# The opening of an expert stage: tokens in weight buffers, small first chunks, other work queued behind the first rows

## The chip, the core and the metric

The kernel runs on one core of a Trainium2 chip. The metric is the device time of one execution in microseconds (us), the median over a few runs. The profile is that of one execution, with its own time beside its span. Engines are named as the profile names them: PE (TensorE matmul) and PEld (its weight loads), DVE (VectorE), ACT (ScalarE), POOL (GpSimd, which issues the gathers) and SP (which issues the other loads).

## The reference, cut to what matters

One token sequence (256 tokens of 1024 features) passes two layers of a mixed attention, recurrence and convolution block and then a third block, which ends with a layer of experts picked per token (`peer` in the reference). Only that last layer is touched:

```
h2 = rmsnorm(x, g_norm2) * (1 + sc2) + sh2                    # normed tokens
q = (h2 @ w_pq) -> 8 heads x 2 halves x 128;  s = q . sub_keys # scores, 128 keys per half
sv, si = top_k(s, 16);  best, pos = top_k(sv0 + sv1, 16)       # 16 experts of 16384 for each token and head
g = softmax(best);  a = gelu(expert_u[eidx] . h2)
x = x + gt2 * sum over heads and experts of g * a * expert_v[eidx]
```

Each token picks 8 x 16 experts, and each expert is a row of `expert_u` and one of `expert_v`, 1024 numbers each, laid side by side in one table `uv`.

## The kernel before, in words

The tokens are two blocks b of 128. A "row" is one gather: for head h, block b and rank k it fetches one `uv` row of 8 KB for each of the 128 tokens, 1 MB, into one of NG = 9 buffers `G` (L1685, POOL). There are 16 rounds r of 16 rows, 256 rows in all: first the eight heads of block 0, then those of block 1. For each row VectorE takes the dot product of its first half with the tokens `hn[b]` (L1689). After a chunk of rows (four, as a rule) ScalarE takes one gelu (L1693), VectorE multiplies by the gates, and for each row ScalarE makes a diagonal matrix `dg` of the weights (L1702) with which TensorE adds the second half of the row into four PSUM accumulators `vacc`: two matmuls of 512 columns in float32, which the profile records in two passes each. Only then is the row's buffer free for another gather.

The scores of a head (`scores`) are 48 matmuls of normed tokens and weights, both split into a rounded part and a rest (`hh` and `hl`, `wh` and `wl`; three products each); the rounded part is an ACT copy (L323), the rest a subtraction on DVE (L268). Weights come through five raw buffers `w` and three split ones. Head 0's scores are made ahead of the stage. `routing` picks the experts on DVE, in small steps that are slipped in between the dot products (`side`, `nside` steps for each row); that of head 0 and block 0 comes in two parts, so that the first eight rows can be asked for early.

What opens the stage, in `peer`: the first part of `routing(0, 0)`; `normed`, which makes the normed tokens in a gather buffer `G` and splits them into `hh` and `hl`; the rest of that routing; `natural`, which turns the tokens to token order by matmuls of `hh` and `hl` with the identity and copies them to `hn` (both blocks); `scores(1)`; `residual`, which transposes the input `XT` in place for the sum at the end, by way of the four PSUM banks in which `vacc` starts afterwards; and then the rounds, with `scores(r + 2)` ahead of each of the first six.

The order on each engine is a planner's. `at(us)` sets the due time of what follows; the planner plays the program through with its own estimates, and of what is ready on an engine takes the one that is due first, so that work due later fills idle places. `tc.issue_after(x)` puts an instruction behind x in that order. Weight loads are due 25 us and splits 6 us ahead of their matmuls; `first_splits` holds two subtractions behind a given instruction. Each engine then runs its list strictly in order.

## Time and profile before

| | us |
|---|---|
| median of three runs | 1377.39 |
| the runs | 1371.65 to 1379.26 |
| profiled execution | 1375.42 |
| its span | 1373.6 |

| engine | busy us | share of the span |
|---|---|---|
| PE | 1197.5 | 87% |
| DVE | 994.4 | 72% |
| ACT | 533.6 | 39% |
| POOL | 292.5 | 21% |

The page's slices put the stage of the experts in the second half of the span: POOL works only there, and the DMA share is at 9 tenths or more nearly throughout. The gathers move 268.45 MB of 387.64. Shares over the whole span say little of one stage; the rows below are of the stage itself. Times of a row are counted from the start of the span.

### The profile page before, as it was taken

To read this page: it belongs to the slowest core of one execution; us is meant where nothing else is said; L and a number is where in the kernel's file an instruction comes from. 1 tells how busy PE (TensorE), PEld (TensorE's weight loads), DVE (VectorE), ACT (ScalarE), POOL (GpSimd) and SP (SyncE) were. 2 spreads that over 40 slices of the span, in tenths; PEclk is the share of its full clock that TensorE was granted. 3 is DMA by queue.
4 is the path that set the end of the run, shared out by engine and by line. 5 is a ranking of instruction groups with operands and counts; after the bars stand their busy time and mean duration, and the time that the engine had idled before them with its cause. 6 is when DMAs were issued, how large, how long until landed. Compare 5 with 4: busy or idle time off the path is not lost.

```text
span 1373.6 us, 17829 instructions
## 1 busy us (share of the span) xinstructions
PE 1197.5 (87%) x6008; PEld 781.7 (57%) x6008; DVE 994.4 (72%) x2464; ACT 533.6 (39%) x1147; POOL 292.5 (21%) x279
## 2 busy tenths in 40 slices
PE   6999899899979999999889977778787877779877
PEld 5987559798947976758676633343333333323333
DVE  6898865599988676466588777777767677676554
ACT  5535643344755555455444312222222222212211
POOL 0000000000000000000033443434444444444442
PEclk8999999899999999999979999988999999998899
DMA  9587455557413442401399999999999999999996
GB/s 333 196 284 270 157 183 173 196 163 260 139 41 100 154 131 77 153 16 36 108 382 381 376 426 428 425 426 361 427 412 426 427 426 418 423 426 404 421 427 275
DMA packets 71483, 387.64 MB, mean 282 GB/s; under 512 B 8417, under 2 KB 9569, under 8 KB 38370
## 3 DMA queue, kind: packets, MB, share of 16 engines
q0 software_dynamic: 36864, 268.45, 46.9%
q1 hardware_dynamic: 34530, 118.06, 25.4%
q8 instruction: 48, 0.79, 0.2%
q14 instruction: 41, 0.34, 0.1%
HBM read 385.43 MB, written 1.05 MB: 281 GB/s over the span
## 4 chain that ended last, share of the span: by engine, by line
PE 49%; DMA 28%; issue 9%; DVE 8%; POOL 5%; ACT 2%; POOLq 0%; DVEq 0%; SPq 0%; ACTq 0%
DMA G<-uv,eix 23%; PE acc L256 22%; PE acx L256 10%; PE s L256 5%; POOL G L1685 5%; DVE G L1689 3%; PE o L256 2%; DMA wm<-wada 2%; PE c L256 2%; PE c L966 2%; PE t L256 1%; DMA w<-wpq 1%; PE t L259 1%; PE s L412 1%; PE o L645 1%
## 5 line engine op out<-in xcount | busy, mean ns | idle before, releaser
L1689 DVE SCALAR_TENSOR_TENSOR G<-G,hn 128x1024 f32<-128x1024 f32 x256 | 313.4, 1225 | 162.3 <-DMA G<-uv,eix 158.8
L1685 POOL DMA_INDIRECT G<-uv,eix x256 | 284.9, 1113 | 415.6 <-PE o L256 129.5
L323 ACT ACTIVATE wh<-w 128x1024 fp32r<-128x1024 f32 (+2 forms) x140 | 146.4, 1048 | 180.6 <-PE acc L256 111.0
L268 DVE TENSOR_TENSOR wl<-w,wh 128x1024 fp32r<-128x1024 f32 (+2 forms) x140 | 168.8, 1209 | 65.4 <-ACT wh L323 63.8
L256 PE MATMUL t<-G,dg 128*128 128x512 f32 x256 | 149.3, 668 | 62.9 <-ACT dg L1702 62.9
L256 PE MATMUL c<-G,dg 128*128 128x512 f32 x256 | 145.9, 654 | 49.2 <-ACT dg L1702 49.2
L256 PE MATMUL acc<-hh,wh 128*128 128x256 f32 x592 | 173.5, 297 | 6.0 <-ACT hh L468 2.5
L256 PE MATMUL acc<-hh,wl 128*128 128x256 f32 x592 | 173.0, 295 | 2.0 <-DVE wl L268 2.0
L256 PE MATMUL acc<-hl,wh 128*128 128x256 f32 x592 | 164.3, 288 | 1.1 <-DVE hl L268 1.1
L1702 ACT ACTIVATE dg<-cst,w 128x128 f32<-128x128 f32 x256 | 90.1, 395 | 141.7 <-PE acx L256 61.4
L256 PE MATMUL acx<-G,dg 128*128 128x512 f32 x256 | 143.3, 644 | 0.0
L256 PE MATMUL o<-G,dg 128*128 128x512 f32 x256 | 141.1, 635 | 0.0
L1693 ACT ACTIVATE s<-s 128x4 f32<-128x4 f32 (+1 forms) x66 | 13.5, 205 | 306.7 <-DVE G L1689 306.7
L256 PEld LDWEIGHTS t<-G,dg 128*128 128x128 f32 x256 | 50.9, 209 | 142.3 <-ACT dg L1702 87.6
L256 PEld LDWEIGHTS acc<-hh,wh 128*128 128x128 f32 x592 | 115.7, 196 | 14.8 <-issue 4.6
L256 PEld LDWEIGHTS acc<-hh,wl 128*128 128x128 f32 x592 | 115.9, 196 | 8.6 <-issue 4.3
L256 PEld LDWEIGHTS c<-G,dg 128*128 128x128 f32 x256 | 49.5, 206 | 117.0 <-ACT dg L1702 68.5
L262 DVE SCALAR_TENSOR_TENSOR g<-lu,pb,g 128x256 f32<-128x256 f32 x264 | 115.1, 478 | 0.2
L256 PEld LDWEIGHTS acc<-hl,wh 128*128 128x128 f32 x592 | 111.3, 192 | 5.3 <-issue 3.4
L256 PEld LDWEIGHTS acx<-G,dg 128*128 128x128 f32 x256 | 53.5, 209 | 70.7 <-issue 70.7
L256 PEld LDWEIGHTS o<-G,dg 128*128 128x128 f32 x256 | 52.7, 206 | 69.0 <-issue 68.8
L1057 POOL MEMSET lu<- 128x16 f32 x1 | 0.4, 441 | 399.3 <-DVE g L262 399.3
(549 smaller groups left out, 1998.6 us busy)
## 6 DMA issues: line engine op xcount, KB each, us to landing
w<-w SPq DMA_DIRECT2D x64, 512.0 KB, 4.4
wm<-wada SPq DMA_DIRECT2D x40, 512.0 KB, 4.3
wa<-cw SPq DMA_DIRECT2D x16, 512.0 KB, 5.0
w<-woa SPq DMA_DIRECT2D x16, 512.0 KB, 3.5
w<-wpq SPq DMA_DIRECT2D x14, 512.0 KB, 4.5
w<-w2t SPq DMA_DIRECT2D x12, 512.0 KB, 3.5
w<-wob SPq DMA_DIRECT2D x8, 512.0 KB, 3.5
w<-w2v SPq DMA_DIRECT2D x8, 512.0 KB, 3.8
```

Of the source, the lines that this page charges most:

```text
L256: return pe.matmul(out, lhsT, rhs, start=start, stop=stop)
L259: pe.transpose(out, in_, ident)
L262: return (e or dve).scalar_tensor_tensor(out, a, s, b, op0=op0, op1=op1)
L268: return (e or dve).tensor_tensor(out, a, b, op=op)
L323: act.activation(hi, w, AF.Copy)
L412: pe.matmul(acc[j:j + 32], ones[:, 0:32], sq[:, q] if square else srcs[i + q], start=i + q < 4, stop=i + q >= n - 4, tile_position=(0, j))
L645: pe.matmul(hps[32 * j:32 * j + 32], blk[:, q4 * 4 + j], w[:, j], start=q4 == 0, stop=q4 == 3, tile_position=(0, 32 * j))
L966: pe.matmul(acc[32 * j:32 * j + 32], sc[:, k], w[:, j], start=k == 0, stop=k == 7, tile_position=(0, 32 * j))
L1685: pool.indirect_dma_start(out=G, out_offset=None, in_=A["uv"], in_offset=bass.IndirectOffsetOnAxis(ap=eix[b][:, h, k:k + 1], axis=0))
L1689: dot = dve.scalar_tensor_tensor(G[:, 0:D], G[:, 0:D], 1.0, hn[b], op0=mul, op1=mul, accum_out=s[:, j:j + 1])
L1693: act.activation(s[:, 0:n], s[:, 0:n], AF.Gelu)
L1702: act.activation(dg, ident, AF.Copy, scale=w[:, j:j + 1])
```

## The change

`normed` now makes the tokens in two of the raw weight buffers `w` (no gather buffer) and adds the shift in place. `natural(0, tokens)` turns only block 0 for the first rows, by float32 transposes straight from these; block 1 follows at round 3 from `hh` and `hl`, as before. The split into `hh` and `hl` is a step of its own (`halves`): its copies are put behind the last copy of `natural`, its subtractions behind the second dot product. Round 0 has chunks of 2, 2, 4, 4, 4 rows instead of four of 4. `scores(1)` is put behind the last matmul of the first two rows and its two weight splits behind their weights; `scores(2)` is due 20 us after the start of the rounds, where it was due 12 us before. `residual` is done per block, before rounds 2 and 4, through the PSUM banks of the scores. No routing steps stand beside the first two rows, a routing that is unfinished at the end of a round may go on in the next if its head is not the next one, and round 1 has three steps for each row instead of two. `finish` reads the residual in its new layout.

```
@@ -1536,13 +1538,14 @@
         gat = [mk(pp, [128, 8, 16], tag=f"gat{b}") for b in range(2)]
         sca = mk(pp, [128, 7, 2, 2, 128], tag="sca")
 
-        def scores(h, t):
+        def scores(h, t, held=None):
 
             acc = pst("u", [128, 2, T])
             for q in range(2):
                 at(t + 2.6 * q)
                 wh, wl = wsplit(A["wpq"][2 * h + q], [128, 8, 128])
-                mm3(acc[:, q], [(wh[:, k], wl[:, k], hh[:, k], hl[:, k]) for k in range(8)])
+                with tc.issue_after(held.ins) if held else nullcontext():
+                    mm3(acc[:, q], [(wh[:, k], wl[:, k], hh[:, k], hl[:, k]) for k in range(8)])
             at(t + 5.2)
             qs = mk(pp, [128, 2, T], tag="qs", bufs=2)
             act.activation(qs, acc, AF.Copy)
@@ -1559,24 +1562,34 @@
                 dg = mk(pp, [128, 128], tag="dg", bufs=3)
                 ts(dg, ident, rs2[:, b:b + 1], None, mul)
                 mm(bc[:, b * 128:b * 128 + 128], ones, dg, True, True)
-            t = mk(pp, [128, 2 * D], tag="G", bufs=NG).rearrange("p (k t) -> p k t", k=8)
+            t = [mk(wp, [128, 4, 256], tag="w", bufs=NRAW) for _ in range(2)]
             for k in range(8):
-                stt(t[:, k], XT[:, k], mg["pr"][:, k:k + 1], bc, mul, mul)
-                sh = modt[:, 24 + k, 0:1]
-                act.activation(hh[:, k], t[:, k], AF.Identity, bias=sh)
-            for k in range(8):
-                stt(hl[:, k], t[:, k], modt[:, 24 + k, 0:1], hh[:, k].bitcast(F32), add, sub)
-
-        def natural():
-
-            for b in range(2):
-                for d in range(2):
-                    acc = pst("u", [128, 4, 128])
-                    for k in range(4):
+                o = t[k // 4][:, k % 4]
+                stt(o, XT[:, k], mg["pr"][:, k:k + 1], bc, mul, mul)
+                act.activation(o, o, AF.Identity, bias=modt[:, 24 + k, 0:1])
+            return t
+
+        def halves(t, a, d):
+            for k in range(0, 8, 2):
+                src = t[k // 4][:, k % 4:k % 4 + 2]
+                with tc.issue_after(a):
+                    act.activation(hh[:, k:k + 2], src, AF.Copy)
+                with tc.issue_after(d):
+                    tt(hl[:, k:k + 2], src, hh[:, k:k + 2].bitcast(F32), sub)
+
+        def natural(b, t=None):
+
+            bs = slice(b * 128, b * 128 + 128)
+            for d in range(2):
+                acc = pst("u", [128, 4, 128])
+                for k in range(4):
+                    if t is None:
                         for i, x in enumerate((hh, hl)):
-                            last = mm(acc[:, k], x[:, d * 4 + k, b * 128:b * 128 + 128], identr, i == 0, i == 1)
-                    act.activation(hn[b][:, d * 512:d * 512 + 512], acc.rearrange("p a b -> p (a b)"), AF.Copy)
-            return last
+                            mm(acc[:, k], x[:, d * 4 + k, bs], identr, i == 0, i == 1)
+                    else:
+                        tr(acc[:, k], t[d][:, k, bs], ident)
+                copied = act.activation(hn[b][:, d * 512:d * 512 + 512], acc.rearrange("p a b -> p (a b)"), AF.Copy)
+            return copied
 
         def subscores(h, b, p):
             return sca0[:, b, p] if h == 0 else sca[:, h - 1, b, p]
@@ -1655,17 +1668,15 @@
             yield ts(g, g, sm, None, mul)
 
 
-        xn = XT.rearrange("p k t -> p (k t)").rearrange("p (b d) -> p b d", b=2)
-
-        def residual(held):
-            xp = [pst("v", [128, 4, 128]) for _ in range(4)]
-            for b in range(2):
-                for k in range(8):
-                    with tc.issue_after(held.ins):
-                        tr(xp[b * 2 + k // 4][:, k % 4], XT[:, k, b * 128:b * 128 + 128], ident)
-            for i in range(4):
-                act.activation(xn[:, i // 2, (i % 2) * 512:(i % 2) * 512 + 512],
-                               xp[i].rearrange("p a b -> p (a b)"), AF.Copy)
+
+        def residual(b):
+
+            for d in range(2):
+                xp = pst("u", [128, 4, 128])
+                cells = XT[:, 4 * d:4 * d + 4, b * 128:b * 128 + 128]
+                for k in range(4):
+                    tr(xp[:, k], cells[:, k], ident)
+                act.activation(cells, xp, AF.Copy)
 
         vacc = []
         side = []
@@ -1692,17 +1703,26 @@
                     if j == n - 1:
                         act.activation(s[:, 0:n], s[:, 0:n], AF.Gelu)
                         w = mk(pp, [128, 4], tag="w4", bufs=3)
-                        tt(w[:, 0:n], s[:, 0:n], gat[b][:, h, c:c + n], mul)
+                        gated = tt(w[:, 0:n], s[:, 0:n], gat[b][:, h, c:c + n], mul)
                     with tc.issue_after(dot.ins):
-                        for _ in range(nside):
+                        for _ in range(nside if h or b or c else 0):
                             while side and next(side[0], 0) == 0:
                                 side.pop(0)
+                if h == 0 and b == 0 and c == 0:
+
+                    at(t + 6)
+                    halves(tokens, copied.ins, dot.ins)
+                    first_splits.extend([gated.ins] * 2)
                 for j, G in enumerate(rows):
                     dg = mk(pp, [128, 128], tag="dg", bufs=3)
                     act.activation(dg, ident, AF.Copy, scale=w[:, j:j + 1])
                     for d in range(2):
-                        mm(vacc[b * 2 + d], dg, G[:, D + d * 512:D + d * 512 + 512], h == 0 and c + j == 0,
-                           h == 7 and c + j == 15)
+                        last = mm(vacc[b * 2 + d], dg, G[:, D + d * 512:D + d * 512 + 512], h == 0 and c + j == 0,
+                                  h == 7 and c + j == 15)
+                if h == 0 and b == 0 and c == 0:
+                    scores(1, t + 8, last)
+                if h == 0 and b == 0 and c == 4:
+                    scores(2, t + 20)
                 c += n
 
         PICK, NG = 2.5, 9
@@ -1716,17 +1736,13 @@
 
         at(B + 2)
         with tc.issue_after(found.ins):
-            normed()
-        at(B + 7)
+            tokens = normed()
+        at(B + 3)
         with tc.issue_after(found.ins):
             for ins in fast:
                 placed = ins
-        at(B + 8)
-        held = natural()
-        first_splits.extend([found.ins] * 2)
-        scores(1, B + 9)
-        at(B + 16)
-        residual(held)
+        at(B + 4)
+        copied = natural(0, tokens)
 
         gtb = mk(pp, [128, 2, 512], tag="gtb")
         gs = mk(pp, [128, D], tag="gs")
@@ -1749,22 +1765,37 @@
                 o = fin[:, d * 512:d * 512 + 512]
                 tt(o, vacc[b * 2 + d], gtb[:, d], mul)
                 yield 1
-                tt(o, o, xn[:, b, d * 512:d * 512 + 512], add)
+                o4 = o.rearrange("p (k n) -> p k n", k=4)
+                tt(o4, o4, XT[:, 4 * d:4 * d + 4, b * 128:b * 128 + 128], add)
                 nc.sync.dma_start(A["out"][b * 128:b * 128 + 128, d * 512:d * 512 + 512], o)
                 yield 1
 
+        route = {}
         for r in range(16):
-            nxt = [routing(q % 8, q // 8) for q in ((1, 2) if r == 0 else (r + 2,)) if q < 16]
-            side[0:0] = nxt
             if r == 3:
                 side.append(gate_sums())
             if r == 10:
                 side.append(finish(0))
-            if r < 6:
-                scores(r + 2, U0 + 16 * PICK * r - 12)
-            experts(r % 8, r // 8, U0 + 16 * PICK * r, 4 if r == 0 else 2, (4, 4, 4, 4) if r < 15 else (4, 4, 4, 2, 1, 1))
-            at(U0 + 16 * PICK * (r + 1))
-            while side and (side[0] in nxt or r in (6, 12)):
+            for q in (1, 2) if r == 0 else (r + 2,):
+                if q < 16:
+                    route[q] = routing(q % 8, q // 8)
+            side[0:0] = [route[q] for q in (r + 1, r + 2) if q in route]
+            t = U0 + 16 * PICK * r
+            if r in (2, 4):
+                at(t)
+                residual(r // 2 - 1)
+            if r == 3:
+                at(t)
+                natural(1)
+            if 0 < r < 6:
+                scores(r + 2, t - 12)
+            experts(r % 8, r // 8, t, 4 if r == 0 else 3 if r == 1 else 2, (2, 2, 4, 4, 4) if r == 0 else (4, 4, 4, 4) if r < 15 else (4, 4, 4, 2, 1, 1))
+            at(t + 16 * PICK)
+            ahead = route.pop(r + 1, None)
+            for _ in ahead or ():
+                pass
+            side[:] = [x for x in side if x is not ahead and x not in route.values()]
+            while side and r in (6, 12):
                 for _ in side.pop(0):
                     pass
         at(U0 + 16 * PICK * 16 + 20)
```

## Rows read from the trace of the kernel before

**Rows 1.** The page's chain that ended last, shares of the span by engine and line.
```profile
DMA G<-uv,eix 23%; PE acc L256 22%; PE acx L256 10%; PE s L256 5%; POOL G L1685 5%; DVE G L1689 3%; PE o L256 2%; DMA wm<-wada 2%; PE c L256 2%; PE c L966 2%; PE t L256 1%; DMA w<-wpq 1%; PE t L259 1%; PE s L412 1%; PE o L645 1%
```

**Rows 2.** Stretches: us; busy time (instructions) per engine; granted TensorE clock; DMA share; GB/s.
```profile
688.00:704.00 16.00, 10.30 (x45) 9.73 (x45) 15.86 (x53) 5.93 (x15) 8.44 (x8) 0.50 0.98 398
716.00:728.00 12.00, 12.00 (x49) 6.98 (x48) 10.98 (x48) 6.27 (x13) 5.71 (x5) 1.00 0.92 327
744.00:764.00 20.00, 20.00 (x95) 13.10 (x94) 12.87 (x36) 7.01 (x13) 8.33 (x8) 1.00 0.97 374
768.00:780.00 12.00, 12.00 (x49) 7.14 (x49) 9.01 (x25) 3.85 (x9) 4.63 (x4) 1.00 0.81 307
800.00:850.00 50.00, 39.43 (x86) 16.34 (x85) 35.90 (x96) 10.77 (x29) 22.84 (x21) 0.96 1.01 427
920.00:940.00 20.00, 18.18 (x60) 9.72 (x59) 13.57 (x37) 6.63 (x15) 6.97 (x6) 0.91 0.83 323
```

**Rows 3.** Timeline of POOL: start, length, line, operation, [idle before <-releaser]; one row per gather.
```profile
686.95 1.41 POOL L1685 DMA_INDIRECT G<-uv,eix  x1 [35.47 <-PE t L256]
...
704.36 1.18 POOL L1685 DMA_INDIRECT G<-uv,eix  x1 [5.78 <-issue]
...
718.40 1.86 POOL L1685 DMA_INDIRECT G<-uv,eix  x1 [12.86 <-PE o L256]
...
727.29 0.94 POOL L1685 DMA_INDIRECT G<-uv,eix  x1 [0.78 <-DVE sv L1621]
...
734.37 1.55 POOL L1685 DMA_INDIRECT G<-uv,eix  x1 [1.28 <-PE o L256]
```

**Rows 4.** Timeline of DVE, from the first index to that of head 1.
```profile
685.71 0.17 DVE L262 SCALAR_TENSOR_TENSOR eix<-ij 128x8 uint32<-128x8 f32 x1
...
686.19 3.49 DVE L268 TENSOR_TENSOR wl<-w,wh 128x1024 fp32r<-128x1024 f32 x3
...
689.60 0.08 DVE L1620 MATCH_VALUE_LOAD tmp<-sv,cst 128x8 f32 x1
...
690.12 3.21 DVE L262 SCALAR_TENSOR_TENSOR G<-XT,mgpr,t 128x256 f32<-128x256 f32 x8
...
693.64 2.84 DVE L262 SCALAR_TENSOR_TENSOR hl<-G,modt,hh 128x256 fp32r<-128x256 f32 x7
...
701.15 1.22 DVE L1689 SCALAR_TENSOR_TENSOR G<-G,hn 128x1024 f32<-128x1024 f32 x1
...
733.44 0.17 DVE L262 SCALAR_TENSOR_TENSOR eix<-ij 128x16 uint32<-128x16 f32 x1
```

**Rows 5.** Timeline of PE.
```profile
686.13 1.22 PE L256 MATMUL t<-dg,cst 128*128 128x128 f32 x4 [4.10 <-DVE dg L265]
...
702.32 1.06 PE L259 MATMUL o<-cst,XT 128*128 128x128 f32 x4
...
716.25 1.02 PE L256 MATMUL c<-G,dg 128*128 128x512 f32 x2
717.11 1.02 PE L256 MATMUL o<-G,dg 128*128 128x512 f32 x2
...
926.24 1.83 PE L256 MATMUL c<-G,dg 128*128 128x512 f32 x2 [1.13 <-ACT dg L1702]
927.86 1.91 PE L256 MATMUL o<-G,dg 128*128 128x512 f32 x2
929.57 1.21 PE L256 MATMUL c<-G,dg 128*128 128x512 f32 x2
```

**Rows 6.** The chain of waits in order of time, 700 to 716 us: start, length, what.
```profile
704.23 9.10 PE acc L256 x74
```

**Rows 7.** Timeline of ACT.
```profile
720.77 0.60 ACT L1553 ACTIVATE sca<-s 128x512 f32<-128x512 f32 x1 [0.39 <-PE s L256]
...
923.29 0.60 ACT L1548 ACTIVATE qs<-acc 128x512 f32<-128x512 f32 x1 [8.71 <-PE acc L256]
...
925.21 0.21 ACT L1693 ACTIVATE s<-s 128x4 f32<-128x4 f32 x1
```

More of the change, by code (lines that the diff above doesn't have):

```diff
@@ L1 @@
+from contextlib import nullcontext
 import numpy as np
```

## The prediction

> **What bounds the kernel now.** I read the chain of waits first: 23% of the span goes to one transfer, the gather of expert rows, more than to any other line [rows 1]. So I looked at the stage from 687 us on in stretches [rows 2]. Over a long quiet stretch the DMA moves 427 GB/s at a share of 1.01, TensorE has slack (39.43 of 50 us) and VectorE too: the stage runs at the speed of the transfers. 256 gathers of 1.05 MB are not changed by this edit, so time can be won or lost only where the DMA falls below 427. At that rate a stretch of w us at g GB/s loses w x (1 - g/427). Three dips lie in the opening: 716 to 728 at 327 (2.8 us), 744 to 764 at 374 (2.5 us), 768 to 780 at 307 (3.4 us), together 8.7 us. The first stretch, 688 to 704 at 398, loses 1.1 us to the start itself. One more dip comes later, 920 to 940 at 323 (4.9 us).
>
> Why the dips are there is read from the gathers [rows 3]. There are nine buffers, and the normed tokens hold one of them at first. Eight rows go out from 686.95 us on, the ninth at 704.36, and the next only at 718.40, after 12.86 us of waiting for TensorE to be done with row 0; rows 13 to 16 leave from 727.29 to 734.37. TensorE in its turn starts on row 0 at 716.25 [rows 5], though VectorE had its first dot product at 701.15 [rows 4]: in between the scores of heads 1 and 2 run, one stretch of 74 of their matmuls lasting 9.10 us [rows 6].
>
> **The change part by part.** The first gather hangs on the index written at 685.71 [rows 4], which is not touched: no gain, no loss, 0.
>
> *To the first dot product.* Before, three splits of 3.49 us together stand ahead of the normed tokens on VectorE (686.19 to 689.60). Now two of them wait for the first weights. The spread of the norm ends at 686.13 + 1.22 = 687.35 [rows 5], so the eight products (3.21 us, [rows 4]) end at 690.6. If the third split still slips in ahead they end up to 1.2 us later. What is left of the first routing: from 689.60 to 701.15 are 11.55 us, less 3.21 for the products and 3.3 for the eight subtractions (2.84 for seven), so 5.0 us. First dot product: 695.6, against 701.15. The token rows for it need eight transposes (four took 1.06 us at the low clock, [rows 5]) and two copies of 0.60 [rows 7] after the last shift at about 691.1; the second half of them is 1.1 + 0.6, so 692.8: 2.8 us in hand, hidden behind VectorE.
>
> *To the first rows on TensorE.* A chunk of two instead of four: 2 x 1.22 us to 698.0, and from the gelu to the first row matmul 926.24 - 925.21 = 1.0 us [rows 5, 7], so 699.1. A row is four such matmuls recorded in two pairs, 0.86 us apart at full clock (716.25 to 717.11), 1.71 at the low one (927.86 to 929.57), after an idle time two pairs are slow (926.24 and 927.86) [rows 5]. TensorE has little to do from 692 to 699, so I take the first two of four pairs as slow: 2 x 1.71 + 2 x 0.86 = 5.1 us (bounds 3.4 and 6.8). Rows 0 and 1 are done at 704.2; before, at about 719.7.
>
> *Behind them.* The scores of head 1 are 48 matmuls at 9.10/74 = 0.123 us [rows 6], 5.9 us: to 710.1. They need the split tokens: four copies on ScalarE (0.60 each, hidden while it waits for the first dot products) and four subtractions on VectorE. The trace has none of this shape; half of one split (1.16) is 0.6, so 2.4 us, instead of 3.3 before. The lower bound is 2.4 - 3.3 = -0.9 us. Behind them two splits stand, 2.3 us, and the next two dot products behind these, until 705.2: TensorE is busy to 710.1, which hides it. Were that cover gone, 4.7 us would fall on rows 2 and 3, the upper bound. Then rows 2 and 3 (3.4 us, to 713.5), eight small matmuls of head 1's scores (about 1 us, an estimate: 8 x 0.123), the scores of head 2 (5.9 us, to 720.4), rows 4 to 7 (4 x 1.72): 722.1, 723.8, 725.6, 727.3. That frees the buffers for rows 13 to 16. Before they left at 727.29 to 734.37: a lead of 5.2 us at row 13 and 7.1 at row 16, in the middle 6.2.
>
> *Row 16* is head 1's first and needs its routing. Before, from the copy of the scores (720.77, [rows 7]) to the index (733.44, [rows 4]) were 12.7 us. Now the copy comes at 710.1 + 0.6 + 1.0 = 711.7, or 3.4 later if rows 2 and 3 go first, and the index at 724.4 to 727.8. Just in time; 0.5 us at most.
>
> *Moved out of the opening:* the residual's 16 transposes and four copies and half of the token rows, now before rounds 2, 3 and 4. There TensorE has 10 us in 50 free [rows 2]; 0, and what it costs without that cover is the rival on the slow side. The extra gelu of the smaller chunk is 0.21 us on an idle ScalarE [rows 7]. The routings of heads 1 and 2 get 14 times 4 steps beside the dot products instead of 16 times 4; each takes 28, so both still fit: 0. The weight loads of head 2 and later find two of five slots held by tokens until about 701 and shift by some 10 us; their bytes are the same, and head 2's first row is 32 rows off: 0.
>
> *Sum.* The lead replaces starvation as long as there is any: 8.7 us of dips stand behind it, so 6.2 us come out of the stage, some 2 of the first dip (it will not vanish: rows 11 and 12 still wait for the scores) and 4 of the two later ones. Profiled execution 1375.42 (span 1373.6 and 1.8 around it) - 6.2 = 1369.2. The median of the runs, 1377.39, is 2.0 above it: 1371.2. I say 1371.
>
> A rule against it: the Trainium skill ("DMA: Bandwidth & Descriptors", section "Bandwidth") says that for loads from HBM a core's share of about 358 GB/s binds, not the ports' 435. By that figure the three dips would lose only 2.7 us and the change could win no more. The trace disagrees with 427 over 50 us [rows 2], so the sum keeps 427 and that rule gets no chance below.
>
> **The rivals.**
> *The low clock.* TensorE was at 0.50 from 688 to 704 [rows 2], behind an idle time, and matmuls in the place of the tokens' transposes ran there. Take those away and the rows may start cold and stay so through the scores: 1.7 us more for rows 0 and 1 and 5.9 more for the scores, 7.6 in all. That eats the lead: 1377 to 1379. For it: 0.50 for 16 us. Against it: the pair at 929.57 was nearly fast again after two slow ones. The skill ("TensorE: Matmul & The Clock Gate", section "What's actually happening") says that the throttled state is the default and that activity releases it. The trace agrees (0.50 after idling); what it leaves open is how many of the scores are caught.
>
> *All dips go.* If the first pairs are fast and later scores fall between rows, all 8.7 us come back: 1375.42 - 8.7 + 2.0 = 1368.7. If the new order also undoes the jam at 920, 1363.8. For it: every gather that was late in the opening was waited for from TensorE or VectorE, not from memory. Against it: TensorE was packed (12.00 of 12 and 20.00 of 20 us, [rows 2]) and has all five heads' scores to do either way.
>
> *Slower: jams on ScalarE in rounds 2 to 4.* At 923.29 a copy out of PSUM sat 8.71 us at the head of ScalarE's queue waiting for scores on TensorE, and the gelu behind it began only at 925.21 [rows 7]; the stretch lost 4.9 us [rows 2]. The moved residual (twice) and token rows (once) put six such copies, in three places, ahead of gelus, on the two PSUM buffers that the scores use. One jam leaves 6.2 - 4.9 = 1.3 us of gain; from the second on it is a loss, and three cost 14.7: 1371.2 + 14.7 = 1385.9. Against it: each place holds 8 transposes or 16 small matmuls, 1 to 2 us, against 5.9 us of scores.
>
> *It does not do what it says:* the order is written by a planner from its own estimates, and it may pull scores of later heads ahead of rows 2 to 7 all the same. The gathers then leave when they did: 1377.
>
> **How the numbers follow.** The forecast, 1371 (1369 to 1373), 0.42; all dips gone (1364 to 1369) 0.25; low clock (1375 to 1379) 0.15; no change of order 0.08; jams (1381 to 1386) 0.10. What a measurement of this kernel can tell is about 0.5%, 6.9 us. Faster than 1370.5 are the second case and nearly half of the first: 0.45. Slower than 1384.3 is part of the jams and what a bad median adds: 0.09. The rest, 0.46, is within. The range 1364 to 1380 leaves out the jams and the tail of the second case.
>
> **What would show it.** Right: a first dot product near 696, row 0 on TensorE near 699, gathers of rows 13 to 16 from 722 to 727, and over 400 GB/s from 716 to 728. Wrong: those gathers at 727 or later (order, clock), a clock of 0.50 beyond 706 (low clock), gather pauses over 7 us in rounds 2 to 4 behind a ScalarE copy (jams). If the gathers lead by 6 us and the time has not moved, then the dips were not starvation and my first step falls.

## The result, and the profile after

The changed kernel is slower: 1391.21 us (1384.87 to 1399.15 over six runs), where the kernel before had 1376.78 beside it (1371.65 to 1383.34). The ratio is 1.0114, with a 95% interval of 1.0089 to 1.0139. The forecast was 1371, and the range ended at 1380. The profiled execution is the slowest of the six: it took 1399.15 us, its span is 1397.3.

First a correction for reading it. In this execution the first index is written at 693.50 us, 7.8 us later than in [rows 4], although up to 660 us TensorE, VectorE and ScalarE have the same instructions in the same order; the last copy on ScalarE that both have in common starts at 659.92 before and at 667.72 after, so the 7.8 us are older than the first difference. In the first 660 us the granted clock has TensorE at its lower level for 58.0 us, against 41.0. That isn't the whole of it: in the experiments' profiled executions the index came at 685.31 to 693.47, and at 692.59 in e13, which had 44.2 us at the lower level. It is no effect of the change, so from here on times are also given **behind the index**: 693.50 is taken from rows of after, 685.71 from rows of before.

The chain of the page hardly moves ([rows 1]):
```profile
DMA G<-uv,eix 24%; PE acc L258 22%; PE acx L258 10%; POOL G L1696 5%; PE s L258 5%; DVE G L1700 3%; DMA wm<-wada 2%; PE o L258 2%; PE c L258 2%; PE c L968 2%; PE t L258 2%; PE s L414 1%; PE t L261 1%; PE o L647 1%; PE o L813 1%
```
The stretches that answer to [rows 2], each 8 us later; columns as there, the last one is GB/s:
```profile
696.00:712.00 16.00, 6.61 (x12) 2.97 (x13) 15.34 (x40) 11.57 (x23) 9.00 (x8) 0.50 0.98 380
724.00:736.00 12.00, 11.46 (x65) 8.39 (x64) 9.27 (x34) 4.70 (x9) 5.01 (x4) 1.00 1.01 422
752.00:772.00 20.00, 20.00 (x108) 14.24 (x107) 14.89 (x44) 6.70 (x14) 6.49 (x7) 1.00 0.79 305
776.00:788.00 12.00, 11.09 (x50) 6.63 (x48) 11.12 (x30) 4.84 (x10) 4.42 (x3) 1.00 0.75 293
808.00:858.00 50.00, 37.91 (x82) 15.39 (x80) 34.77 (x92) 10.84 (x29) 23.39 (x21) 0.97 1.01 421
928.00:948.00 20.00, 16.48 (x58) 9.21 (x57) 16.57 (x35) 6.44 (x12) 8.15 (x7) 0.91 0.95 381
```
Two things are to be seen. The first dip is gone (327 to 422 GB/s), but the next two are deeper (374 to 305, 307 to 293); the last stretch is better (323 to 381), which says little, as the ledger below shows. And the quiet stretch, which was to stay as it was, runs at 421 instead of 427 with the same DMA share, 1.01.

The gathers on POOL (start, length, operation, idle time before and what ended it), rows 0, 8, 9, 13 to 17, 19 to 21, 24 and 25:
```profile
694.58 1.08 POOL L1696 DMA_INDIRECT G<-uv,eix  x1 [8.42 <-DVE tmp L1633]
...
710.90 2.32 POOL L1696 DMA_INDIRECT G<-uv,eix  x1 [5.17 <-issue]
713.53 0.94 POOL L1696 DMA_INDIRECT G<-uv,eix  x1 [0.30 <-issue]
...
730.29 1.72 POOL L1696 DMA_INDIRECT G<-uv,eix  x1 [5.39 <-DVE si L1635]
732.32 1.46 POOL L1696 DMA_INDIRECT G<-uv,eix  x1 [0.30 <-issue]
734.08 0.94 POOL L1696 DMA_INDIRECT G<-uv,eix  x1 [0.30 <-issue]
742.12 1.19 POOL L1696 DMA_INDIRECT G<-uv,eix  x1 [7.10 <-PE acc L258]
752.44 0.93 POOL L1696 DMA_INDIRECT G<-uv,eix  x1 [9.14 <-PE o L258]
...
755.87 1.06 POOL L1696 DMA_INDIRECT G<-uv,eix  x1 [0.56 <-PE o L258]
759.03 0.94 POOL L1696 DMA_INDIRECT G<-uv,eix  x1 [2.09 <-PE o L258]
768.04 0.94 POOL L1696 DMA_INDIRECT G<-uv,eix  x1 [8.08 <-DVE G L1700]
...
774.63 0.94 POOL L1696 DMA_INDIRECT G<-uv,eix  x1 [2.22 <-PE o L258]
782.97 1.60 POOL L1696 DMA_INDIRECT G<-uv,eix  x1 [7.41 <-PE o L258]
```
Row 9 leaves 20.0 us behind the index (718.40 in [rows 3] is 32.7), row 13 36.8 (41.6). But row 16 leaves at 48.6 (48.7 before: 734.37 in [rows 3]), and pauses of 9.14, 8.08 and 7.41 us follow. The bracket of row 16 names PE, but the buffer that it needs was free from 737.8 on, when row 7's last matmul ended; it waited for its index, written at 741.18. Rows 17 to 20 leave when they did before, to 0.1 us; row 21 is the first that leaves later, 74.5 us behind the index (69.2 before). Rows 17, 20 and 21 of the kernel before:
```profile
744.62 0.94 POOL L1685 DMA_INDIRECT G<-uv,eix  x1 [8.70 <-PE o L256]
...
751.20 0.94 POOL L1685 DMA_INDIRECT G<-uv,eix  x1 [2.21 <-PE acc L256]
...
754.96 0.94 POOL L1685 DMA_INDIRECT G<-uv,eix  x1 [2.81 <-PE o L256]
```

A ledger shows where the transfers lost time. For stretches of 20 us from the index on, each loses 20 x (1 - g/427); as g comes in whole GB/s, an entry is good to some 0.2 us. MB are all that the DMA moved from the index to the end of the span.

| kernel | lost us, 0 to 120 | 120 to 260 | 260 to 660 | MB in the stage |
|---|---|---|---|---|
| before | 12.4 | 5.5 | 4.8 | 278.7 |
| after | 15.9 | 4.9 | 10.9 | 279.8 |
| e2 (buffers aligned) | 15.7 | 3.6 | 3.1 | 279.8 |
| e3 (before, buffers shifted) | 13.1 | 3.4 | 11.5 | 278.7 |
| e4 (moved steps held) | 10.9 | 14.1 | 8.4 | 279.8 |
| e5 (moved steps far later) | 13.8 | 7.8 | 3.2 | 279.9 |
| e6 (scores in pieces) | 19.5 | 12.3 | 4.1 | 279.8 |
| e8 (e5, copies behind gelu) | 8.4 | 2.3 | 4.7 | 279.8 |
| e9 (before, copies behind gelu) | 9.0 | 3.3 | 4.0 | 278.8 |
| e10 (e5, routing later) | 10.5 | 5.2 | 3.2 | 279.8 |
| e11 (e8, tokens in G) | 8.4 | 2.6 | 5.0 | 278.8 |

After against before has three entries: 3.5 us in the opening, 6.1 us spread over the 400 us from 260 to 660, and 1.05 MB more, which is 2.5 us at 427 GB/s. How far single executions can be trusted is seen from the seven that have the order of after (after, e1, e2, e7 and e12 to e14): the opening loses 15.6 to 16.8 us in them, the second stretch 3.6 to 8.2, most of that between 240 and 260 (352 GB/s in e2, 254 in e12). So the first column can be read to about a microsecond, the second can't.

### The profile page after: what moved, and what is told of

It reads as the page before. It is cut to its first block, busy times and chain, and to the rows that moved or that the text cites. A ratio compares the mean times of both kernels' runs of the same rounds, so it can differ in the third digit from the quotient of the medians.

```text
span 1397.3 us, 17805 instructions
## 1 busy us (share of the span) xinstructions
PE 1197.2 (86%) x6000; PEld 779.0 (56%) x6000; DVE 993.4 (71%) x2461; ACT 534.8 (38%) x1152; POOL 298.6 (21%) x279
## 3 DMA queue, kind: packets, MB, share of 16 engines
q0 software_dynamic: 36864, 268.45, 46.8%
HBM read 385.43 MB, written 1.05 MB: 277 GB/s over the span
## 4 chain that ended last, share of the span: by engine, by line
PE 49%; DMA 27%; issue 8%; DVE 8%; POOL 5%; ACT 2%; POOLq 0%; DVEq 0%; SPq 0%; ACTq 0%
DMA G<-uv,eix 24%; PE acc L258 22%; PE acx L258 10%; POOL G L1696 5%; PE s L258 5%; DVE G L1700 3%; DMA wm<-wada 2%; PE o L258 2%; PE c L258 2%; PE c L968 2%; PE t L258 2%; PE s L414 1%; PE t L261 1%; PE o L647 1%; PE o L813 1%
## 5 line engine op out<-in xcount | busy, mean ns | idle before, releaser
L1696 POOL DMA_INDIRECT G<-uv,eix x256 | 291.1, 1137 | 395.5 <-PE o L258 150.0
L1704 ACT ACTIVATE s<-s 128x4 f32<-128x4 f32 (+2 forms) x67 | 13.7, 204 | 312.8 <-DVE G L1700 312.8
```

Source lines behind the costliest of these rows:

```text
L1696: pool.indirect_dma_start(out=G, out_offset=None, in_=A["uv"], in_offset=bass.IndirectOffsetOnAxis(ap=eix[b][:, h, k:k + 1], axis=0))
```

## The experiments

**e1, the change again.** No edit.

> The changed kernel once more, on the chip that runs the next three. Order theory (the planner pulled the residual, the token rows of block 1 and later heads' scores in among the first 16 rows, 6.5 us) and placement theory (the gather buffers now begin 32 bytes past a multiple of 64, so every gather lands more slowly, some 8 us over 256) together: 1.010 to 1.012 of before, gathers 2.48 us apart in the last 100 us, 421 GB/s in quiet stretches. Variation theory (the slower transfers of the one profile were that chip's or that execution's): 1.004 to 1.006, 2.43 us, 427 GB/s.

1389.78 us (1388.03 to 1390.53), ratio 1.0106 (1.0085 to 1.0126). That is what the two theories of order and address give together. It is the reference for e2.

**e2 and e3, the address of the gather buffers.** The quiet stretch was slower with no change of work in it. What did change is where the nine buffers `G` lie: at 135168 + n x 8192 bytes of a partition before, at 146592 + n x 8192 after, because before `normed` allocated the first of them ahead of the small tiles of `routing`. 135168 is a multiple of 4096; 146592 is 32 past a multiple of 64. e2 aligns the changed kernel, e3 shifts the kernel before by 32 bytes; the order of instructions is the same as without the pad.
```
e2, ahead of the first G:  + mk(pp, [128, 216], tag="pad")    # G at 147456
e3, ahead of normed's G:   + mk(pp, [128, 8], tag="pad")      # G at 135200
```


> The changed kernel with 864 unused bytes ahead of the gather buffers, so that they begin on a multiple of 4096 as before; the order of every engine is the same. Placement theory: gathers 2.43 us apart and 427 GB/s again, 7 to 9 us less than the changed kernel on this chip (ratio to before 1.003 to 1.006). Order and variation theories: no change against the changed kernel (within 2 us).

> The kernel before with 32 unused bytes ahead of the gather buffers, nothing else. Placement theory: gathers 2.48 us apart, 421 GB/s, 7 to 9 us slower than before (1.005 to 1.007). Order and variation theories: 1.000 within 0.002, 2.43 us.

The stretch from 800 to 850 us in e2, then in e3:
```profile
800.00:850.00 50.00, 40.43 (x82) 16.63 (x80) 35.22 (x95) 10.94 (x30) 22.69 (x22) 0.90 1.01 426
```
```profile
800.00:850.00 50.00, 38.46 (x82) 15.74 (x82) 34.81 (x96) 10.76 (x29) 23.67 (x21) 0.95 1.01 420
```
The rate follows the address both ways. e2 took 1384.93 us (ratio 1.0076, 1.0052 to 1.0101), 4.9 under e1; e3 1386.16 (1.0084, 1.0062 to 1.0106), 11.7 over before. The sign is as expected in both, the size (7 to 9 us) in neither. At 421 instead of 427 GB/s the 268.45 MB of gathers take 9.0 us more, between the two. The packets of 8 KB tell the same: 309 ns from the 5th to the 95th percentile in before and e2, a median of 311 and 313 and a 95th percentile of 321 and 320 in after and e3.

**e7, e12, e13, e14, how much alignment.** The changed kernel with pads of 32, 352, 96 and 224 bytes.

> The changed kernel with 32 bytes more ahead of its gather buffers, which puts them on a multiple of 64 bytes but of no larger power of two (146624 + n x 8192). If it is lines of 64 bytes that count, the quiet stretch runs at 426 to 427 GB/s as in the kernel before and e2, packets of the gathers are 279 to 280 ns in the mean. If a larger multiple is needed, 420 to 422 GB/s and 283 to 284 ns as in the changed kernel.

> The changed kernel with 352 bytes more ahead of its gather buffers, which puts them on a multiple of 512 bytes but of no larger power of two (146944 + n x 8192). If a multiple of 512 is enough, the quiet stretches run at 426 to 428 GB/s and the packets of the gathers have a median of 309 ns, as in the kernel before (multiple of 4096) and e2; if a larger one is needed, 420 to 422 GB/s and 311 to 313 ns as in the changed kernel and e7.

> The changed kernel with 96 bytes more ahead of its gather buffers: a multiple of 256 bytes and of no larger power of two (146688 + n x 8192). The Trainium skill (DMA: Bandwidth & Descriptors, section How a descriptor splits into AXI transactions) says that a transaction has to start on a boundary of 256 bytes. By that rule this one is as fast as e12: 426 to 428 GB/s in quiet stretches, packets of the gathers 309 ns in the median and up to the 95th percentile. Rival (512 are needed): 420 to 422 GB/s, 311 to 313 ns, 320 at the 95th percentile.

> The same with 224 bytes: a multiple of 128 and of no larger power of two (146816 + n x 8192). By the rule of 256 bytes it is as slow as the changed kernel and e7: 420 to 422 GB/s, 311 to 313 ns in the median, 320 at the 95th percentile. Rival (128 are enough): 426 to 428 GB/s and 309 ns.

The stretch from 850 to 900 us, in the order 64, 128, 256, 512:
```profile
850.00:900.00 50.00, 39.28 (x78) 15.82 (x76) 37.54 (x93) 9.92 (x26) 21.14 (x20) 0.89 1.01 421
```
```profile
850.00:900.00 50.00, 36.40 (x76) 15.19 (x76) 36.10 (x89) 10.90 (x29) 22.10 (x20) 0.93 1.01 421
```
```profile
850.00:900.00 50.00, 37.48 (x75) 15.21 (x73) 37.95 (x94) 9.52 (x25) 19.85 (x19) 0.90 1.01 426
```
```profile
850.00:900.00 50.00, 39.05 (x78) 15.89 (x77) 37.50 (x94) 10.73 (x29) 21.22 (x20) 0.90 1.01 426
```
64 and 128 are slow (95th percentile of the packets 320 and 321 ns), 256 and 512 are fast (309). So the boundary lies at 256 bytes, and all sixteen traces agree: the ten with `G` on a multiple of 256 have 309 ns, the six without have 320 or 321. How far past the boundary makes no difference: 32 (e3), 128 (e14), 160 (after) and 192 bytes (e7) all give 420 to 421 GB/s. The Trainium skill ("DMA: Bandwidth & Descriptors", section "How a descriptor splits into AXI transactions") says of what a transaction reads that it has to start on a 256-byte boundary, and counts the extra ones for an unaligned descriptor. The traces show the same boundary for the SBUF address that a gather writes to, and the price: 1.4% of the rate at 8 KB rows. Single times of these four runs (1386.89 to 1392.23) are too few to compare.

**e4, the moved steps held back.** The traces show that the planner drew the moved steps forward: the two halves of the residual run ahead of rows 8 and 16, the token rows of block 1 ahead of row 12, where TensorE is full. e4 puts each behind the last row of the round before the one it was written for.
```
  def residual(b, held): ...
+     with tc.issue_after(held):
          tr(xp[:, k], cells[:, k], ident)
  (natural(1) likewise; held = last matmul of the round before)
```


> The changed kernel with the transposes of the residual and the matmuls of block 1's token rows put behind the last matmul of the round before theirs, so that the planner cannot pull them into the first 16 rows (heads 4 and 5's scores, which use the same two PSUM buffers in turn, are held back with them). Order theory: gathers of rows 21 to 60 come 4 to 7 us earlier than in the changed kernel, and the time is 4 to 7 us less. Placement theory alone: within 2 us of the changed kernel. A rival inside the order theory, jams: each of the three places becomes a lump of 6 to 8 us of TensorE work ahead of rows, the DMA falls below 400 GB/s there, and nothing is won.

1397.26 us, ratio 1.0168 (1.0137 to 1.0198): slower still. The opening gains 5.0 us in the ledger, but 120 to 260 loses 14.1. At rows 32 and 48 the held steps stand in a lump with the scores of heads 4 and 5, which wait for the same two PSUM buffers; 10.4 of the 14.1 us, however, stand from 220 to 260, behind row 64, where copies of scores wait 7.55 us (to 909.50) and 5.60 us (to 937.27) at the head of ScalarE's queue.

**e5, the moved steps far later.** e2 with `natural(1)` ahead of round 6 and `residual` ahead of rounds 8 and 9.
```
- if r in (2, 4): residual(r // 2 - 1)       + if r in (8, 9): residual(r - 8, ends[-1])
- if r == 3: natural(1)                      + if r == 6: natural(1, None, ends[-1])
```


> The changed kernel with its gather buffers on multiples of 4096 bytes (as e2), and the moved steps far later: natural(1) ahead of round 6, residual ahead of rounds 8 and 9, each behind the last matmul of the round before it, so that none of them stands among rows 0 to 20; the scores are left as the planner puts them. Order theory (the moved steps, which the planner drew into the opening between rows 8 and 16, make the gathers of rows 21 to 64 late): row 36 goes out some 4 to 8 us earlier than in e2 (115.6 us behind the first index there, 107.4 before), row 64 at 178 instead of 182, and the time is 3 to 5 us under e2, 1380 where e2 had 1385. Rival (the scores of later heads, 48 matmuls in a block, make them late): rows 21 to 48 stay within 2 us of e2 and the time too, 1385.

1382.24 us, ratio 1.0047 (1.0028 to 1.0066), 0.3% under e2. The time is nearly as the order theory had it, but the two intervals overlap, and in the traces the whole stage isn't shorter (695.0 us from the index to the end of the span; 690.9, 692.8 and 696.4 in e2, e13 and e12). Shown is an opening that loses 1.9 us less, not that the time falls. Of the forecast way, too, only half came true. Row 32 left 97.9 us behind the index (103.0 in e2, 100.5 before), row 36 at 113.8 (115.6): the gain was lost again between row 32 and row 33, in a pause of 9.32 us.

**e6, scores in four pieces**: e5 with the scores of heads 3 to 7 in four pieces, each behind a chunk of rows.
```
+ with tc.issue_after(held[2 * q + j]): mm3(...)     # 12 matmuls, held = last matmul of a chunk
```


> e5 with the scores of heads 3 to 7 cut into four pieces of 12 matmuls, each behind a chunk of rows of the round before. If blocks of score matmuls between rows are what starves the gathers, the stretches under 400 GB/s between row 8 and row 64 go, row 36 leaves 100 to 104 us behind the first index (107.4 before), the stage is 4 to 8 us shorter than in the kernel before, and the time is 1366 to 1371 where before has 1374.5. Rival (TensorE is packed there whatever the order, and the DMA waits for the sum of its work): row 36 within 2 us of e5, time within 3 us of e5. Rival on the slow side: a piece that waits for its weights holds up the rows behind it, and the time is over e5.

1396.48 us, ratio 1.0161 (1.0136 to 1.0186): the rival on the slow side, with the split of the weights in the place of their load. ScalarE waits 7.44 us, to 750.39, with a weight split for a slot that the held matmuls still read, VectorE 4.67 us for that split, and TensorE 5.58 us for the rows behind it.

**What e5 and e6 have in common**, an instruction at the head of ScalarE's queue that waits for TensorE, is seen in the changed kernel itself. The rows are of ScalarE, VectorE and TensorE, in this order:
```profile
767.87 0.40 ACT L1718 ACTIVATE dg<-cst,w 128x128 f32<-128x128 f32 x1 [2.60 <-PE o L258]
774.75 0.60 ACT L1551 ACTIVATE qs<-acc 128x512 f32<-128x512 f32 x1 [6.49 <-PE acc L258]
775.25 0.59 ACT L1679 ACTIVATE XT<-acc 128x512 f32<-128x512 f32 x1
775.72 1.06 ACT L325 ACTIVATE wh<-w 128x1024 fp32r<-128x1024 f32 x1
776.67 0.60 ACT L1556 ACTIVATE sca<-s 128x512 f32<-128x512 f32 x1
777.15 0.61 ACT L1679 ACTIVATE XT<-acc 128x512 f32<-128x512 f32 x1
777.78 1.28 ACT L1704 ACT_TABLE_LOAD   x1
779.22 0.20 ACT L1704 ACTIVATE s<-s 128x4 f32<-128x4 f32 x1 [0.16 <-DVE G L1700]
```
```profile
776.82 1.23 DVE L270 TENSOR_TENSOR wl<-w,wh 128x1024 fp32r<-128x1024 f32 x1 [6.18 <-ACT wh L325]
777.96 1.22 DVE L1700 SCALAR_TENSOR_TENSOR G<-G,hn 128x1024 f32<-128x1024 f32 x1
```
```profile
774.55 0.60 PE L261 MATMUL acc<-cst,XT 128*128 128x128 f32 x4
775.40 1.16 PE L258 MATMUL s<-sk,qs 128*128 128x128 f32 x8 [0.25 <-ACT qs L1551]
776.40 0.60 PE L261 MATMUL acc<-cst,XT 128*128 128x128 f32 x4
780.82 1.02 PE L258 MATMUL c<-G,dg 128*128 128x512 f32 x2
```
The copy `qs` (head 5's scores) sits at the head of ScalarE's queue for 6.49 us, until TensorE has made the scores. Behind it stands the split `wh`; VectorE, in order too, waits 6.18 us for it with the subtraction, and behind that stands the dot product of row 19, 84.5 us behind the index where before had 74.9. Then the gelu, then the row at 780.82, and only then the gather at 782.97. Before has such waits too ([rows 7], 8.71 us), but fewer in the opening; after has 5.77 us at 759.38, this one, and 6.64 us at 798.89, and e5 has 6.65 us at the place where its lead was lost.

**e8 and e9, the copies behind a gelu.** The copies of the scores of heads 3 to 7 are put behind the gelu of a round's third chunk, in e5 (giving e8) and in the kernel before (giving e9); the routing of a head moves one round later for that, and in e8 round 1 has two routing steps for each row again instead of three.
```
- act.activation(qs, acc, AF.Copy)            # in scores(h)
+ if c == 8 and waiting:                      # in experts, behind that chunk's gelu
+     copies(*waiting.pop(), t + PICK * 12 + 6, gelu.ins)
```


> e5 with one thing more: the copy of the scores of heads 3 to 7 out of PSUM (qs) no longer stands where the planner likes on ScalarE, but behind the gelu of the third chunk of a round, when TensorE has long made them; the routing of a head moves one round later for that. Theory (ScalarE sits at the head of its queue on such a copy for 5 to 7 us in three places between rows 12 and 28 of the changed kernel, weight splits, dot products and the gelu wait behind it, and the rows with them): the pauses of the gathers at rows 20 to 21, 24 to 25 and 32 to 33 shrink from 7 to 10 us to under 5, row 36 leaves 100 to 106 us behind the first index (115.6 in e2, 113.8 in e5, 107.4 before), less than 11 us of DMA time is lost in the first 128 us (15.8 in e2, 12.5 before), and the time is 1368 to 1375. Rival (the blocks of 48 score matmuls themselves starve the gathers, wherever the copy stands): row 36 at 112 or later, time 1380 to 1385 as in e2 and e5.

> The kernel before with the same edit as e8: the copies of the scores of heads 3 to 7 behind the gelu of a round's third chunk, the routing of a head one round later. Theory: its jams on ScalarE (5.06 us at 764.71, 2.40 and 3.86 at 778 and 784, 8.71 at 923.29) go, 4 to 8 us of the time with them: 1367 to 1371. Against e8 it tells what the new opening itself is worth once neither has jams: if the opening saves what the prediction said, e8 is 4 to 6 us faster than e9; if TensorE, which sits idle for 7 us before the first row in the new opening, pays for it behind, e8 and e9 are within 3 us, or e9 is faster.

e8 took 1375.32 us, ratio 0.9985 (0.9967 to 1.0004); e9 1372.41, ratio 0.9966 (0.9947 to 0.9985). In e8 none of the five moved copies waits; the first of them, with the gelu ahead of it, on ScalarE:
```profile
784.06 0.21 ACT L1718 ACTIVATE s<-s 128x4 f32<-128x4 f32 x1 [4.90 <-DVE G L1714]
784.17 0.58 ACT L1561 ACTIVATE qs<-acc 128x512 f32<-128x512 f32 x1
```
The opening loses 8.4 us instead of 13.8. Row 36 left at 107.9, not at the 100 to 106 that I expected, and the time is 0.3 us over the upper end: more waits than these remain. e9 missed its range (1367 to 1371) by 1.4 us. The better half of the answer is e9 all the same: without the waits the kernel before gains as well, and the new opening is then no faster than the old one.

**e10, the control.** e8 also moved the routing. e10 is e5 with that alone (and the two steps in round 1).

> The control to e8: e5 with the routing of a head one round later, as in e8, but with the copies of the scores left where the planner puts them. If e8 won by the copies (jams on ScalarE), this one jams as e5 does: 13 to 15 us of DMA time lost in the first 120 us behind the first index (13.8 in e5, 8.4 in e8), about 8 in the 140 us behind them, and a time of 1380 to 1384 where before has 1376 to 1377. If it was the later routing, the time is 1374 to 1377 as in e8.

1380.57 us, ratio 1.0033 (1.0014 to 1.0051): near e5 (1.0047), over e8 (0.9985). The time came as the copies' theory had it; the loss in the ledger did not (10.5 us in the opening, where 13 to 15 was expected), so part of what e8 gained there is likely the routing's. The copies are shown to be worth the step from e10 to e8 (1.0033 to 0.9985, intervals apart); the step from e5 to e10 is within the intervals.

**e11, tokens in a gather buffer again.** e8, with `normed` writing into a `G` as before.
```
- t = [mk(wp, [128, 4, 256], tag="w", bufs=NRAW) for _ in range(2)]
+ t = mk(pp, [128, 2 * D], tag="G", bufs=NG).rearrange("p (a k t) -> p a k t", a=2, k=4); t = [t[:, 0], t[:, 1]]
```


> e8 with the normed tokens back in a gather buffer instead of two weight buffers (the pad goes; G on multiples of 4096). In the changed kernel two tiles of weights more have to be loaded while the gathers run (279.6 to 280.1 MB between the first index and the end, 278.6 to 278.8 MB with the tokens in G): 1.05 MB at 427 GB/s, 2.5 us. Theory: the stage moves 278.6 MB again and is 2 to 3 us shorter than e8's (683.7 us), near e9's 681.8; row 8 leaves some us later, hidden. Rival (those loads fall into stretches in which the DMA waits anyway): stage and time as e8, 1375.

The stage moves 278.8 MB again and takes 681.1 us (683.7 in e8). The time is 1372.10, ratio 0.9975 (0.9953 to 0.9997); the gain over e8 is within the intervals, and single stages of one order (e2, e12) differ by 5.5 us, so the 1.05 MB are shown and their 2.5 us are not, though stage and medians fit them. e9 and e11 are faster than both kernels, by 0.34% and 0.25% of before.

## Why the prediction was wrong, step by step

- *First dot product, 9.9 us behind the index.* Early by 1.6: 8.3, at 701.82.
- *Rows 0 and 1, 5.1 us at mixed clock.* Right: 708.75 to 713.69, 4.9 us. They started 15.3 us behind the index, not 13.4. From the first dot product to row 0 were 6.9 us, not 3.5: a table load of 1.28 us on ScalarE (705.01) stood ahead of the gelu, and on VectorE the four subtractions of the split ahead of the product with the gates (707.64).
```profile
708.75 2.08 PE L258 MATMUL c<-G,dg 128*128 128x512 f32 x2 [8.18 <-ACT dg L1718]
710.61 1.92 PE L258 MATMUL o<-G,dg 128*128 128x512 f32 x2
712.32 1.08 PE L258 MATMUL c<-G,dg 128*128 128x512 f32 x2
713.24 1.02 PE L258 MATMUL o<-G,dg 128*128 128x512 f32 x2
713.69 0.68 PE L258 MATMUL acc<-hh,wh 128*128 128x256 f32 x1
```
What I didn't price is the 8.18 us ahead of them: TensorE does nothing there, while before it turned tokens and made scores ahead of row 0 (one stretch of 9.10 us of them, [rows 6]). The scores come behind instead, and TensorE has no idle time in the second dip (20.00 of 20 us). What this costs was not measured by itself.
- *Rows 13 to 16 with a lead of 5 to 7 us.* Right for rows 13 to 15 (36.8, 38.8 and 40.6 us behind the index, forecast 36.4 to 39.9). Wrong for row 16, forecast 41.6.
- *Row 16's index "just in time" at 724.4 to 727.8.* **This step failed first.** That is 38.7 to 42.1 us behind the index; it came at 47.7, exactly as before, so the lead was 0 from row 16 on, and with it went the 6.2 us of the sum. The term was wrong in two places. The copy `sca` of head 1's scores, forecast 26.0 to 29.4 us behind the index, began at 32.6: row 0 had started 1.9 us late, and besides rows 2 and 3 (which the 29.4 allows for) 12 matmuls of head 2, 1.8 us, stood ahead of head 1's small matmuls on TensorE (724.97). From the copy to the index were 15.1 us where the sum had before's 12.7: four weight splits of later heads were slipped in between the steps on VectorE, none before. TensorE, ScalarE, then VectorE:
```profile
724.97 1.06 PE L258 MATMUL s<-sk,qs 128*128 128x128 f32 x8
```
```profile
726.06 0.60 ACT L1556 ACTIVATE sca<-s 128x512 f32<-128x512 f32 x1 [5.17 <-PE s L258]
```
```profile
726.69 0.49 DVE L1629 MAX8 sv<-sca 128x8 f32<-128x128 f32 x2 [2.67 <-ACT sca L1556]
...
728.20 1.21 DVE L270 TENSOR_TENSOR wl<-w,wh 128x1024 fp32r<-128x1024 f32 x1
...
729.99 1.21 DVE L270 TENSOR_TENSOR wl<-w,wh 128x1024 fp32r<-128x1024 f32 x1
...
731.71 1.22 DVE L270 TENSOR_TENSOR wl<-w,wh 128x1024 fp32r<-128x1024 f32 x1
...
737.44 1.22 DVE L270 TENSOR_TENSOR wl<-w,wh 128x1024 fp32r<-128x1024 f32 x1
...
741.18 0.17 DVE L264 SCALAR_TENSOR_TENSOR eix<-ij 128x16 uint32<-128x16 f32 x1
```
This explains the gain that did not come, not the loss: row 16 leaves 48.6 us behind the index in e8 as well, whose opening loses less than before's. The loss sets in at row 21.
- *The residual and the token rows "moved out of the opening", 0.* Wrong. They were not moved out: the planner fills idle places with what is due later, and it put them ahead of rows 8, 12 and 16. With them held or far later the opening loses 5.0 (e4) and 1.9 us (e5) less; that the time as a whole falls is not shown, since what e4 gains it loses again behind row 64, and e5's 0.3% is within the intervals. That I named this planner's habit as a reason for no change, and then took the moved steps as gone, was a contradiction in the working.
- *Weight loads: "their bytes are the same".* Wrong where it matters. 1.05 MB, two tiles of 512 KB, moved from ahead of the index, where the DMA had room (108 GB/s in the page's slice from 652 to 687 us before), into the stage that it bounds: 2.5 us by 427 GB/s. e11 takes the bytes back.
- *The quiet stretch at 427.* The premise that nothing but dips could change failed: the addresses of the gather buffers, 9.0 us by the rates, 4.9 and 11.7 by e1 against e2 and e3 against before. No row of before could show it; the order of allocation in the diff could.
- *The rivals.* "Jams on ScalarE" was given 0.10 and is the mechanism that the experiments show, in rounds 0 and 1 rather than 2 to 4, and behind scores rather than the moved steps. That its 1385.9 is near the 1384.9 of e2, the kernel without the address effect, is luck: it is made of three jams of 4.9 us and has nothing for the bytes. "Low clock" did not happen: the pairs of row 1 were fast again, and the clock granted from 713.70 to 720.10, where head 1's scores ran, was 1.00. "All dips go" did not happen either.

The sum, in its own terms: instead of -6.2 in the opening +3.3 (e2; +3.5 in after), +2.5 for the bytes, and the addresses. These can be taken from the stages of the seven executions of this order: 690.9, 692.8 and 696.4 us where `G` is aligned (e2, e13, e12) and 698.1 to 703.8 where it isn't (e14, e1, e7, after), 693.4 and 700.0 in the mean, so 6.6 us. Together 12.4; the stages say 12.1 (before, one execution, has 687.9), and the medians differ by 14.4. For e2 the fit is worse: 5.8 by the sum, 10.4 by the medians. What is missing there may lie ahead of the index, where executions differ by 8.2 us; that is not shown.

e8 has the bytes and the alignment of e2 and none of its loss, so what e2 loses can be won back by the order alone. But the same edits win 5.2 us in the kernel before (e9), so this doesn't tell how much of e2's loss the new order caused. Which of its waits costs how much is not settled, and neither is why the new opening gains nothing once the waits are gone: it loses 8.4 us in e8's ledger and 9.0 in e9's, and e8 takes 2.9 us longer, for which the bytes (2.5 us) would nearly be enough. An order with head 1's routing kept free of splits was not tried.

## What to carry to other kernels

A head start is worth only what the last of its followers makes of it: follow it to the first row that depends on something else (here the next head's index), and look there before anything is counted. In an order that a planner writes, work that is moved later returns into the idle places of its estimate, and a copy out of PSUM that it puts ahead of a gelu can hold up three engines when its estimate is short (6.49 us on ScalarE and 6.18 on VectorE here, with a row on TensorE behind them): hang such copies behind work that is certainly later. And whenever a change allocates tiles in another order, compare the addresses of the buffers that the DMA fills, before the trace is blamed.

## What was not expected of the hardware

- Gathers of 8 KB rows into buffers that lie off a multiple of 256 bytes in SBUF run at 420 to 421 GB/s instead of 426 to 427; the profile's DMA share is 1.01 in both, so only the GB/s and the packets' times show it.
- The same instructions in the same order reached the first index between 685.31 and 693.50 us, with 8.2 us between executions, more than the 6.2 us that were forecast; times behind a common event of the trace could still be compared.
